# A hybrid decoder layer on one core: the last supertile's gates, keys and mix ahead of the output products, and its output norm by halves

## The chip, the core and the metric

The kernel runs on one core of a Trainium2 chip. The metric is the device time of one launch in microseconds (us). TensorE (PE, with its weight loads as PEld), VectorE (DVE), ScalarE (ACT), GpSimd (POOL) and the DMA queue of SyncE (SP) each work through a list of instructions in a fixed order; semaphores make one engine wait for another. A profiled execution gives start, duration and waits of every instruction.

## The reference

One layer on x of 4096 tokens by 1024 features. From a modulated RMSNorm h, one projection feeds sliding-window attention (window 128), RWKV-7 time mixing and gated linear attention; each is multiplied by its SiLU gate, and the three side by side are the mix.

```python
h = _rmsnorm(x, g_pre) * (1.0 + scale[:, None]) + shift[:, None]
proj = h @ w_in
...
attn = attn * jax.nn.silu(ag)
...
rwkv = rwkv * jax.nn.silu(rg)
gla = _gla_mixer(h, gq, gkk, gv, gk1, gk2, gk_b, gla_norm_w) * jax.nn.silu(gg)
y = jnp.concatenate([attn, rwkv, gla], axis=-1) @ w_out
return x + gate[:, None] * _rmsnorm(y, g_post)
```

## The kernel before

The sequence is cut into NS = 16 supertiles of NT = 256 tokens. A first phase computes h, the RWKV and the linear-attention part and stores them in device memory (hscr, mscr). The second phase, which the change touches, makes attention, gates, mix and output for each supertile i. Products of full precision are split in a high and a low float16 half, and three products of halves stand for one.

The stages of the second phase are Python generators:

- `qkv(i)` projects keys (`kp`), queries (`qp`, two tiles) and values (`vp`) from h (tile `hT`, two buffers).
- `gates(i)` makes four gate tiles (`gp`), 48 matmuls each, and writes tanh and product into the one tile `ag`.
- `stage_s(i)` is the attention in two halves of 128 tokens: scores `sc`, softmax in `pr`, a transpose on DVE, and `ovp`, 40 small matmuls for each group, copied to `mxa`.
- `stage_m(i)` loads the other half of the mix (`mxb` from mscr), multiplies both by the gates, squares them on ACT for a common power-of-two scale (sums by the small matmul `mp`, result `msc`, `oi`), and splits seven combinations of the mix into `block`s. A block is one ACT and one DVE instruction of 512 columns, into one of four slots of `mtp` in turn.
- `outp(i)` runs seven products of 12 matmuls of 512 columns (a seven-product scheme for a two by two block product). Product n reads block n and a weight: four stay in SBUF (`o`), three (n = 0, 3, 6) share `ov`, which is loaded again during the product that reads it, by two DMAs issued after its 6th and 12th matmul. `add` on DVE combines the results from PSUM (tag `pj`, two banks, shared with the projections) into `yv`.
- `norm(i, a, ...)` squares 1024 columns on ACT, takes the inverse root on DVE in small one-column steps, scales, adds x and stores 128 tokens.

`stage_p2(i)` strings them together: outp(i-1), gates(i), load of h, qkv(i+1), and for i = 15 also outp(15). So gates(15) came after outp(14), and outp(15) came when all was done but its own mix. `stage_m(i)` waited until outp(i-1) was emitted as a whole.

The class `Order` notes every instruction with the tiles it reads and writes. Its `pin` then plans the order on each engine by a model of durations: whatever is ready and has the lowest rank (program order, with add and the PSUM read-outs lifted by URGENT = 150) goes next. That order is fixed in the program. The chip follows it, whatever the durations turn out to be.

Where the profile names L334, it is the one line of the class `Lane` through which every operation is issued, so tiles tell operations apart.

Of the kernel before, what the change touches and what calls it, by code (L numbers as in the profile page):

```python
# [21 lines left out]
P = 128  # L22
D = 1024
T = 4096
NT = 256
NS = T // NT
# [9 lines left out]
URGENT = 150  # L36
# [362 lines left out]
def hybrid_kernel(ctx, tc, x, vecs, rows, ada1, adaw, w1, wl, w2, wo, w2aug, a2, gk2, cst, ctr, ctg, abias, out):  # L399
    nc = tc.nc  # L400
    model = Model(tc)
    V = Lane(model, nc.vector, *LANES[0])
    S = Lane(model, nc.scalar, *LANES[1])
    G = Lane(model, nc.gpsimd, *LANES[2])
    PE = Lane(model, nc.tensor, *LANES[3], serial=True)
    SP = Lane(model, nc.sync, *LANES[4])

    def pool_of(at, name, bufs=1, **kw):
        return model.order.pool(at.enter_context(tc.tile_pool(name=name, bufs=bufs, **kw)), bufs)
# [4 lines left out]
    st = pool_of(ctx, "small", 3)  # L414
# [13 lines left out]
    magic = cp.tile([P, 16], I32, name="magic")  # L428
# [60 lines left out]
    def pjt(name):  # L489
        return pst("pj", name, 2)  # L490
# [4 lines left out]
    def mq(name):  # L495
        return pst("mq", name)
# [52 lines left out]
    done = set()  # L549
# [95 lines left out]
    with ExitStack() as p1:  # L645
# [155 lines left out]
        for n in range(2 * KD):  # L801
            k, half = n // 2, n % 2
# [978 lines left out]
    def block(i, n):  # L1781

        f = F[i]
        t = blocks[len(split) % len(blocks)]
        split.append((i, n))
        f["blk"].append(t)
        S.activation(t[:, 0], f["src"][n], AF.Identity, scale=f["msc"])
        V.scalar_tensor_tensor(t[:, 1], f["src"][n], f["msc"], t[:, 0], op0=ALU.mult, op1=ALU.subtract)

    def stage_m(i):  # L1790

        yield [("s", i), ("gates", i), ("o", i - 1)]
        f = F[i]
        ag, half = f["ag"], [f["mx"], wt([P, 4, NT], "mxb", 1)]
        SP.dma_start(half[1].rearrange("p b n -> p (b n)"), mscr[i])
        yield [*half, ag]
        mss = st.tile([P, 2], F32, tag="mss", name="mss")
        f["blk"] = []
        for j in range(2):
            for n in (2 * j, 2 * j + 1):  # L1800
                z = half[j][:, 2 * (n % 2) : 2 * (n % 2) + 2, :].rearrange("p b n -> p (b n)")
                V.scalar_tensor_tensor(z, z, g_h[n], ag[:, 2 * n : 2 * n + 2, :].rearrange("p b n -> p (b n)"),
                                       op0=ALU.mult, op1=ALU.mult)
            S.activation(blocks[(len(split) + j) % len(blocks)].rearrange("p a k n -> p (a k n)"),
                         half[j].rearrange("p k n -> p (k n)"), AF.Square, accum_out=mss[:, j : j + 1])
# [12 lines left out]
        (a11, a21), (a12, a22) = [[h[:, :, t * P : (t + 1) * P] for t in range(2)] for h in half]  # L1818
        s1 = wt([P, 4, P], "sm1", 1)
        f["src"] = [a11, a12, a11, s1, a21, a22, a12]  # L1820
        V.tensor_tensor(s1, a21, a22, op=ALU.add)
        V.tensor_tensor(a21, a11, a21, op=ALU.subtract)
        yield [msc]
        block(i, 0)
        V.tensor_tensor(a11, s1, a11, op=ALU.subtract)
        block(i, 1)
        V.tensor_tensor(a12, a12, a11, op=ALU.subtract)
        yield [a11]
        for n in range(2, len(blocks)):
            block(i, n)  # L1830

    def load_o(t, n):
# [3 lines left out]

    PRODUCTS = ((0, False), (1, True), (6, True), (3, False), (4, True), (5, True), (2, False))

    def outp(i):
# [5 lines left out]
        yv = [wt([P, D], "yv", 2) for _ in range(2)]  # L1845
        c1, c2 = slice(0, 512), slice(512, 1024)

        def product(po, n):
            yield [f["blk"][n]]
            A, (w, stays) = f["blk"][n], PRODUCTS[n]  # L1850
            W = Wr[w] if stays else Wv
            for k in range(KD // 2):
                for a, b in ((0, 0), (0, 1), (1, 0)):
                    PE.matmul(po, A[:, a, k, :], W[:, k, :, b, :], start=k == a == b == 0,
                              stop=k == KD // 2 - 1 and a == 1)
                if k == 1 and not stays:
                    later = [m for m, s in PRODUCTS[n + 1 :] + PRODUCTS[: n + 1] if not s][0]
                    if n < 6 or i < NS - 1:
                        SP.dma_start(Wv[:, 0:2], woscr[later, :, 0:2])
                if k == 3 and not stays and (n < 6 or i < NS - 1):  # L1860
                    SP.dma_start(Wv[:, 2:4], woscr[later, :, 2:4])
                yield
            if n + len(blocks) < 7:
                block(i, n + len(blocks))

        def full(n):
            yield ["pj"]
            po = pjt("op")
            yield from product(po, n)
# [8 lines left out]
        yield from full(0)  # L1878
        model.order.urgent = URGENT
        S.copy(y21, f["po"])  # L1880
        model.order.urgent = 0
        yield from full(1)
        add(y11, y21)
# [5 lines left out]
        add(y22, y12)  # L1889
        add(y21, y21)  # L1890
        yield from full(5)
        add(y21, y21)
        norm(i, 1, yv[1], x2[:, 0:D], f["blk"][5])
        if i < NS - 1:
            SP.dma_start(x2[:, 0:D], x[i * NT : i * NT + P, :])
        else:
            SP.dma_start(x2[:, D : 2 * D], x[i * NT : i * NT + P, :])
        yield from full(6)
        add(y12, y12)
        norm(i, 0, yv[0], x2[:, 0:D] if i < NS - 1 else x2[:, D : 2 * D], f["blk"][6])  # L1900
        done.add(("o", i))

    def norm(i, a, yv, xt, junk):
        oi = F[i]["oi"]
        sy = st.tile([P, 1], F32, tag="sy", name="sy")
        S.activation(junk.rearrange("p a k n -> p (a k n)"), yv, AF.Square, scale=oi, accum_out=sy)
        V.tensor_scalar(sy, sy, 1.0 / D, 1e-6, op0=ALU.mult, op1=ALU.add)
        ry = st.tile([P, 1], F32, tag="ry", name="ry")
        rsqrt(ry, sy, 1)
        V.tensor_mul(ry, ry, oi)  # L1910
        V.scalar_tensor_tensor(yv, yv, ry, gn, op0=ALU.mult, op1=ALU.mult)
        V.tensor_add(yv, yv, xt)
# [197 lines left out]
```

## Time and profile before

| | |
|---|---|
| runs of the kernel | 2110.41, 2110.42, 2101.18 us, median 2110.41 |
| profiled execution | 2094.68 us, of it the span 2092.9 us |
| mean granted clock of PE | 0.98 |
| one supertile in steady state | 62.5 us |
| DVE busy | 1613.3 us, 77% of the span |

The profile's page gives busy times over the span; the stages differ, so the end of the run has to be read in windows of its own. One supertile of the second phase repeats with little change, as the chain of work that ended last shows in order of time (start, duration, engine, tile): two scores, the products, ovp, gates, ovp, gates, keys, queries.

```profile
1949.62 5.61 PE op L334 x26
1955.23 0.87 PE sc L334 x8
1956.10 8.20 PE op L334 x38
1964.30 1.36 PE ovp L334 x78
1967.51 1.29 PE op L334 x6
1968.80 11.90 PE gp L334 x109
1980.70 1.36 PE ovp L334 x78
1982.06 9.17 PE gp L334 x83
1991.23 2.62 PE kp L334 x24
1993.85 5.25 PE qp L334 x48
```

All steps but a few are PE's. The chain follows the wait that ended last, so the engines not in it had finished earlier.

### The profile page before, as it was taken

Reading aid. Unit: us, or ns where it says so; the run is one execution under the profiler, and the core shown is the slowest. Engines: PE = TensorE matmul, PEld = TensorE weight load, DVE = VectorE, ACT = ScalarE, POOL = GpSimd, SP = SyncE. Lnnn points to the kernel's source line nnn. Section 1 sums busy time; section 2 is a strip of 40 time slices with the busy share of each in tenths; the row PEclk is TensorE's granted clock in tenths of the full one; section 3 lists DMA queues with packets and bytes.
Section 4 is the critical chain, followed back from the end, with each engine's and each line's share of the span. In section 5 each row is a group of like instructions: output and inputs, shape, how many; then the busy total and the mean of one; then the engine's idle time right before and its main releaser. Section 6 shows DMA issues by size and latency. Waiting matters only on the chain. (4 is left out here: it accounts for less than half of the span.)

```text
span 2092.9 us, 61576 instructions
## 1 busy us (share of the span) xinstructions
PE 1957.4 (94%) x24931; PEld 1517.7 (73%) x24931; DVE 1613.3 (77%) x5214; ACT 1152.2 (55%) x2758; POOL 214.3 (10%) x403
## 2 busy tenths in 40 slices
PE   5899999999999999999876999999999999999996
PEld 2678777787787778777666677777787777787773
DVE  5777888878877688988736878877778877777876
ACT  4867676576776766765334444443444453444442
POOL 0520111421111112101100000000000000000000
PEclk9999999999999999999988999999999999999998
DMA  8432233323323322445034434333334343334341
GB/s 328 137 94 78 74 105 98 92 91 109 97 81 116 102 66 66 116 152 166 20 90 161 154 122 144 105 129 110 124 112 144 106 135 105 122 112 144 116 133 71
DMA packets 183606, 241.95 MB, mean 116 GB/s; under 512 B 52163, under 2 KB 141716, under 8 KB 179094
## 3 DMA queue, kind: packets, MB, share of 16 engines
q1 hardware_dynamic: 183174, 237.45, 35.2%
q8 instruction: 197, 3.23, 0.7%
q14 instruction: 91, 0.75, 0.1%
q10 hardware_dynamic: 144, 0.52, 0.1%
HBM read 177.08 MB, written 60.82 MB: 114 GB/s over the span
## 5 line engine op out<-in xcount | busy, mean ns | idle before, releaser
L334 PEld LDWEIGHTS <-mtp 128*128 128x128 f16 x1344 | 130.4, 98 | 142.5 <-issue 3.8
L334 PE MATMUL op<-o,mtp 128*128 128x512 f16 x768 | 171.9, 380 | 0.0
L334 ACT ACTIVATE pr<-pr,nm,lsc 128x256 f32<-128x256 f32 (+1 forms) x256 | 149.2, 585 | 36.7 <-DVE nm L334 36.7
L334 PE MATMUL op<-ov,mtp 128*128 128x512 f16 x576 | 144.9, 381 | 2.1 <-ACT mtp L334 2.1
L334 PEld LDWEIGHTS <-hT 128*128 128x128 f16 x1536 | 119.4, 100 | 25.4 <-issue 4.0
L334 DVE TENSOR_TENSOR yv<-op,yv 128x512 f32<-128x512 f32 x112 | 75.1, 681 | 56.6 <-PE op L334 41.3
L334 DVE CUSTOM_DVE_ANT_0 pr<-sc,ab,sinks 128x256 f32<-128x256 f32 (+1 forms) x256 | 107.8, 475 | 8.8 <-PE sc L334 6.0
L334 ACT ACTIVATE mtp<-yv,oi 128x1024 f16<-128x1024 f32 x32 | 36.6, 1144 | 126.7 <-DVE yv L334 125.2
L334 PE MATMUL pv<-gvh,hT 128*128 128x272 f16 x512 | 99.4, 285 | 6.1 <-DVE kg L334 3.0
L334 ACT ACTIVATE ag<-gp,gh 128x512 f32<-128x512 f32 x64 | 43.7, 683 | 106.6 <-PE gp L334 106.6
L334 POOL COPY kT<-kT 128x512 f16<-128x512 f16 x15 | 9.7, 647 | 869.8 <-DVE kT L334 820.4
L334 PE MATMUL lp<-hT,Lh 128*128 128x256 f16 x512 | 92.4, 274 | 0.1
L334 PE MATMUL gp<-hT,q3h 128*128 128x256 f16 x512 | 87.1, 275 | 4.3 <-PEq L1967 3.9
L334 DVE SCALAR_TENSOR_TENSOR ag<-ag,gp 128x512 f32<-128x512 f32 x64 | 43.8, 685 | 61.3 <-ACT ag L334 61.3
L334 PE MATMUL gp<-hT,q5h 128*128 128x256 f16 x512 | 90.1, 277 | 0.1
L334 PE MATMUL zz<-hT,vh 128*128 128x256 f16 x512 | 88.8, 273 | 1.3 <-DVE zb L334 1.3
L334 PE MATMUL zz<-hT,kh 128*128 128x256 f16 x512 | 89.8, 273 | 0.0
L334 PE MATMUL zz<-hT,rh 128*128 128x256 f16 x512 | 89.8, 275 | 0.0
L334 PE MATMUL gqk<-hT,gqkh 128*128 128x256 f16 x512 | 89.6, 276 | 0.0
L334 PE MATMUL qp<-hT,q0h 128*128 128x256 f16 x512 | 85.3, 273 | 2.3 <-DVE yv L334 1.5
L334 PE MATMUL qp<-hT,q1h 128*128 128x256 f16 x512 | 86.2, 273 | 0.0
L334 PE MATMUL gp<-hT,q4h 128*128 128x256 f16 x512 | 85.2, 273 | 0.0
(438 smaller groups left out, 6029.4 us busy)
## 6 DMA issues: line engine op xcount, KB each, us to landing
ov<-woscr SPq DMA_DIRECT2D x96, 512.0 KB, 3.9
xt<-in_x SPq DMA_DIRECT2D x16, 1024.0 KB, 5.0
hscr<-hT SPq DMA_DIRECT2D x16, 1024.0 KB, 5.4
hT<-hscr SPq DMA_DIRECT2D x16, 1024.0 KB, 4.8
out<-yv SPq DMA_DIRECT2D x32, 512.0 KB, 2.9
x<-in_x SPq DMA_DIRECT2D x30, 512.0 KB, 4.3
cs<-in_w SPq DMA_DIRECT2D x112, 128.0 KB, 2.3
v<-vscr SPq DMA_DIRECT2D x128, 64.0 KB, 2.5
```

The lines of the kernel that those rows point to most:

```text
L334: r = f(*args, **kw)
```

## The change

The order of stages is changed for the last supertiles only. stage_p2(14) runs outp(13), qkv(15), gates(14); stage_p2(15) runs gates(15), outp(14), outp(15). stage_m(15) waits for the mix of 14 and not for all products of 14; before its blocks it waits for the products of 14 whose slots it takes. It gets buffers that are free by then: `mxe` in a slot of hT in place of mxb, `pr` tiles for the squares, and `q` tiles in place of yv. outp(15) runs product 1 ahead of product 0 and makes blocks 4 and 5 after product 0.

The last norm is rewritten. `last_square` squares 512 columns as soon as they are complete and multiplies them by gn at once. `last_norm` takes the inverse root with two small instructions for a step in place of three, scales and adds x by halves of 512 columns, and stores four pieces in place of two. For the second 128 tokens (h = 1) the scaling is on ACT and the add of x on POOL.

```diff
-        yield [("s", i), ("gates", i), ("o", i - 1)]
+        yield [("s", i), ("gates", i), ("o" if i < NS - 1 else "m", i - 1)]
         f = F[i]
-        ag, half = f["ag"], [f["mx"], wt([P, 4, NT], "mxb", 1)]
+        ag, half = f["ag"], [f["mx"], wt([P, 4, NT], "mxb", 1) if i < NS - 1 else
+                              t_hT("mxe").rearrange("p a k n -> p (a k n)").bitcast(F32)[:, 0 : 4 * NT].rearrange("p (b n) -> p b n", b=4)]
...
+        def last(n):
+            return [(f"o{n}", i - 1)] if i == NS - 1 else []
...
-        yield [msc]
+        yield [msc, *last(3)]
         block(i, 0)
         V.tensor_tensor(a11, s1, a11, op=ALU.subtract)
+        if i == NS - 1:
+            yield last(4)
         block(i, 1)
...
+            if i == NS - 1:
+                yield last(n + 3)
             block(i, n)
...
+    def last_square(f, h, part, sums):
+
+        z = f["end"][h]
+        cols = slice(part * 512, part * 512 + 512)
+        S.activation(f["junk"][:, 0:512], f["yv"][h][:, cols], AF.Square, scale=f["oi32"], accum_out=sums[:, part : part + 1])
+        V.tensor_tensor(z[:, cols], f["yv"][h][:, cols], gn[:, cols], op=ALU.mult)
+
+    def last_norm(f, h, sums, xt):
+
+        v, y, t = [st.tile([P, 1], F32, tag=f"ln{n}", name=f"ln{n}") for n in range(3)]
+        V.scalar_tensor_tensor(v, sums[:, 0:1], 1e-6, sums[:, 1:2], op0=ALU.add, op1=ALU.add)
+        V.tensor_single_scalar(t.bitcast(I32), v.bitcast(I32), 1, op=ALU.logical_shift_right)
+        V.tensor_tensor(y.bitcast(I32), magic[:, 0:1], t.bitcast(I32), op=ALU.subtract)
+        for c in (3.0, 12.0, 768.0):
+            V.scalar_tensor_tensor(t, y, y, v, op0=ALU.mult, op1=ALU.mult)
+            V.scalar_tensor_tensor(y, t, -c, y, op0=ALU.add, op1=ALU.mult)
+        V.scalar_tensor_tensor(y, y, -1.0 / 8192, f["oi"], op0=ALU.mult, op1=ALU.mult)
+        z, r0 = f["end"][h], (NS - 1) * NT + h * P
+        for cols in (slice(0, 512), slice(512, 1024)):
+            if h:
+                S.activation(z[:, cols], z[:, cols], AF.Identity, scale=y)
+                G.tensor_tensor(z[:, cols], z[:, cols], xt[:, cols], op=ALU.add)
+            else:
+                V.scalar_tensor_tensor(z[:, cols], z[:, cols], y, xt[:, cols], op0=ALU.mult, op1=ALU.add)
+            SP.dma_start(out[r0 : r0 + P, cols], z[:, cols])
...
-            if n + len(blocks) < 7:
-                block(i, n + len(blocks))
+            for m in ((4, 5), ())[n] if i == NS - 1 and n < 2 else (n + len(blocks),) if n + len(blocks) < 7 else ():
+                block(i, m)
+            done.add((f"o{n}", i))
...
+        first = [(y21, 0)] if not end else [(y11, 1), (y21, 0)]
+        for y, n in first:
+            yield from full(n)
+            model.order.urgent = URGENT
+            S.copy(y, f["po"])
+            model.order.urgent = 0
+        if end:
+            add(y11, y11)
+            last_square(f, 0, 0, sums[0])
...
-        if i == 1:
+        if i in (1, NS - 1):
             yield from gates(i)
         if i > 0:
             yield from outp(i - 1)
-        if i > 1:
+        if i == NS - 2:
+            yield from qkv(i + 1)
+        if 1 < i < NS - 1:
             yield from gates(i)
```

Where the order moves, first on PE, before, at the start of the last products (op is a product's PSUM tile, q6l the low half of a gate weight, gp of 15):

```order
L334 MATMUL gp_33795<-hT_32198,q6l_18742 128x256
L334 MATMUL mp_33857<-mss_33850,ones_64 128x2
L334 LDWEIGHTS mtp_21671
L334 MATMUL op_33889<-ov_19576,mtp_21671 128x512
L334 LDWEIGHTS mtp_21671
```

The same place with the change: the end of gates(15), then, where the dots are, the first two products of supertile 14, and the mp of 15.

```order
L334 MATMUL gp_33638<-hT_32198,q6l_18742 128x256
L334 LDWEIGHTS mtp_21671
L334 MATMUL op_33694<-ov_19576,mtp_21671 128x512
...
L334 MATMUL op_33721<-o1_19572,mtp_21671 128x512
L334 MATMUL mp_33728<-mss_33705,ones_64 128x2
L334 LDWEIGHTS mtp_21671
L334 MATMUL op_33757<-o6_19573,mtp_21671 128x512
```

So mp of 15 stood alone between the last gate and the first product; now it stands between products 1 and 2 of supertile 14.

Next DVE after outp(13), at the softmax of 14's second half, as a piece of the difference (pr is the softmax tile, kT and kp the keys of 15, q and qp its queries, sy the norm's sum):

```order
 L334 TENSOR_TENSOR yv<-yv,x_21670 128x1024
+L334 SCALAR_TENSOR_TENSOR kT<-kp,kq_s,kT 64x256 x4
 L334 TENSOR_TENSOR sm<-sm,es 128x8
 L334 RECIPROCAL rd<-sm 128x8
-L334 TENSOR_SCALAR pr<-pr,rd 128x256 x4
-L334 SCALAR_TENSOR_TENSOR ag<-ag,gp 128x512
-L334 TENSOR_SCALAR pr<-pr,rd 128x256 x4
+L334 TENSOR_SCALAR sy<-sy 128x1
+L334 TENSOR_SCALAR pr<-pr,rd 128x256 x8
 L334 STREAM_TRANSPOSE pr<-pr 128x1024 x2
+L334 SCALAR_TENSOR_TENSOR q<-qp,q 64x512
```

The keys moved ahead of the softmax's scaling, and the queries behind its transposes.

Last DVE with the change between the products of 14 and of 15 (yv_33693 and 33692 are the halves of 14 in its norm, q_33889 and q_33890 those of 15, op_33912 is product 0 of 15 and op_33935 its product 2):

```order
L334 SCALAR_TENSOR_TENSOR mtp_21671<-sm1_33745,msc_33732,mtp_21671 128x512
L334 SCALAR_TENSOR_TENSOR yv_33693<-yv_33693,ry_33827,x2_21670 128x1024
L334 SCALAR_TENSOR_TENSOR nwt_33869<-nwt_33869,sy_33864 128x1
L334 SCALAR_TENSOR_TENSOR mtp_21671<-mxe_33690,msc_33732,mtp_21671 128x512
L334 TENSOR_TENSOR yv_33693<-yv_33693,x2_21670 128x1024
L334 SCALAR_TENSOR_TENSOR ry_33867<-nwt_33869,ry_33867 128x1
L334 TENSOR_TENSOR nwt_33869<-ry_33867 128x1
L334 SCALAR_TENSOR_TENSOR nwt_33869<-nwt_33869,sy_33864 128x1
L334 SCALAR_TENSOR_TENSOR mtp_21671<-mxa_33048,msc_33732,mtp_21671 128x512
L334 TENSOR_TENSOR q_33889<-op_33912,q_33889 128x512
```

The blocks and adds of 15 now stand among the norms of 14, which before lay under the gates of 15. Between the seventh add of 14 and the add of op_33912 there are 23 rows; these nine are the last, and the 14 ahead of them are one more block (of mxa) and 13 rows of one column.

On SP the load of `mxe` now waits for gates(14) to have read hT, the two loads of x for the end wait for gates(15), and the loads of ov stand behind them. The store of 14's second half stands ahead of the ov loads of 15's last product.

More of the change, by code (lines that the diff above doesn't have):

```diff
@@ L1803, in stage_m @@
                                        op0=ALU.mult, op1=ALU.mult)
-            S.activation(blocks[(len(split) + j) % len(blocks)].rearrange("p a k n -> p (a k n)"),
-                         half[j].rearrange("p k n -> p (k n)"), AF.Square, accum_out=mss[:, j : j + 1])
+            if i < NS - 1:
+                junk = blocks[(len(split) + j) % len(blocks)].rearrange("p a k n -> p (a k n)")
+            else:
+                junk = wt([P, 4, 256], "pr", 3).rearrange("p j n -> p (j n)").bitcast(F16)[:, 0:D]
+            S.activation(junk, half[j].rearrange("p k n -> p (k n)"), AF.Square, accum_out=mss[:, j : j + 1])
         done.add(("og", i))
@@ L1837, in hybrid_kernel @@
     PRODUCTS = ((0, False), (1, True), (6, True), (3, False), (4, True), (5, True), (2, False))
+    def last_square(f, h, part, sums):
[17 more added lines that the diff above has]
+                G.tensor_tensor(z[:, cols], z[:, cols], xt[:, cols], op=ALU.add)
+            else:
+                V.scalar_tensor_tensor(z[:, cols], z[:, cols], y, xt[:, cols], op0=ALU.mult, op1=ALU.add)
+            SP.dma_start(out[r0 : r0 + P, cols], z[:, cols])
     def outp(i):
@@ L1844, in outp @@
         yield [("m", i)]
-        yv = [wt([P, D], "yv", 2) for _ in range(2)]
+        yv = [wt([P, D], "yv", 2) if i < NS - 1 else
+              wt([P, 2, 4, NT], "q", 2, F16).rearrange("p a b n -> p (a b n)").bitcast(F32) for _ in range(2)]
         c1, c2 = slice(0, 512), slice(512, 1024)
@@ L1877, in outp @@
         (y11, y12), (y21, y22) = [[y[:, c1], y[:, c2]] for y in yv]
[L1878 to L1883, printed above, removed]
+        end = i == NS - 1
+        if end:
+            f["yv"], (f["junk"], *f["end"]) = yv, [wt([P, 4, 256], "pr", 3).rearrange("p j n -> p (j n)") for _ in range(3)]
+            oi32 = f["oi32"] = st.tile([P, 1], F32, tag="oi32", name="oi32")
+            V.tensor_single_scalar(oi32, f["oi"], 1.0 / 32, op=ALU.mult)
+            sums = [st.tile([P, 2], F32, tag="lsum", name="lsum") for _ in range(2)]
+        first = [(y21, 0)] if not end else [(y11, 1), (y21, 0)]
[4 more added lines that the diff above has]
+            model.order.urgent = 0
+        if end:
+            add(y11, y11)
+            last_square(f, 0, 0, sums[0])
+        else:
+            yield from full(1)
+            add(y11, y21)
         yield from full(2)
@@ L1889, in outp @@
         add(y22, y12)
+        if end:
+            last_square(f, 1, 1, sums[1])
         add(y21, y21)
@@ L1892, in outp @@
         add(y21, y21)
-        norm(i, 1, yv[1], x2[:, 0:D], f["blk"][5])
-        if i < NS - 1:
+        if end:
+            last_square(f, 1, 0, sums[1])
+            last_norm(f, 1, sums[1], x2[:, 0:D])
+            SP.dma_start(x2[:, D : 2 * D], x[i * NT : i * NT + P, :])
+        else:
+            norm(i, 1, yv[1], x2[:, 0:D], f["blk"][5])
             SP.dma_start(x2[:, 0:D], x[i * NT : i * NT + P, :])
-        else:
-            SP.dma_start(x2[:, D : 2 * D], x[i * NT : i * NT + P, :])
         yield from full(6)
         add(y12, y12)
-        norm(i, 0, yv[0], x2[:, 0:D] if i < NS - 1 else x2[:, D : 2 * D], f["blk"][6])
+        if end:
+            last_square(f, 0, 1, sums[0])
+            last_norm(f, 0, sums[0], x2[:, D : 2 * D])
+        else:
+            norm(i, 0, yv[0], x2[:, 0:D], f["blk"][6])
         done.add(("o", i))
```

## The prediction

> **What bounds the kernel now.** I read the page first, then the last 125 us as windows, then the waits in them, then single rows. The first two lines are the page's; in the windows the columns are length, then busy time and instructions of each engine, then TensorE's granted clock.
>
> ```profile
> span 2092.9 us, 61576 instructions
> PE 1957.4 (94%) x24931; PEld 1517.7 (73%) x24931; DVE 1613.3 (77%) x5214; ACT 1152.2 (55%) x2758; POOL 214.3 (10%) x403
> ```
> ```profile
> 1968.64:2031.12 62.48, 61.60 (x640) 46.93 (x639) 48.88 (x136) 27.98 (x71) 0.00 (x0) 1.00 0.37 121
> 2031.12:2053.70 22.58, 22.58 (x273) 19.79 (x271) 17.93 (x49) 9.88 (x28) 0.00 (x0) 1.00 0.33 113
> 2053.70:2059.83 6.13, 0.60 (x3) 0.50 (x3) 4.11 (x14) 2.61 (x5) 0.00 (x0) 0.68 0.00 0
> 2059.83:2079.56 19.73, 19.73 (x84) 8.42 (x84) 10.65 (x18) 5.78 (x9) 0.00 (x0) 0.93 0.32 106
> 2079.56:2092.90 13.34, 0.00 (x1) 0.00 (x0) 8.77 (x29) 1.24 (x2) 0.00 (x0) 0.64 0.19 79
> ```
> ```profile
> PE mp L334 <- ACT mtp L334: 3.5, 1, 3.5
> PE op L334 <- ACT mtp L334: 2.1, 1, 2.1
> PE sc L334 <- DVE m L334: 0.9, 1, 0.9
> ```
>
> PE bounds the run: up to 2053.70 it is busy all the time but 0.9 us. Then supertile 15 has nothing to hide behind: PE stands for 6.13 us while the mix is formed, runs the 84 product matmuls, and the last 13.34 us are norm and store with PE empty. The change can gain only in these three stretches; elsewhere PE's work is the same, since both kernels have the same matmuls and the orders agree up to 1968.64, where product 6 of supertile 13 has been issued.
>
> **The change, part by part.**
>
> *1. The gap in front of the products.* Product 0 of 15 now comes after the products of 14, during which stage_m(15) runs. PE keeps only the small product mp, 0.14 us between busy neighbours: 6.13 − 0.14 = **6.0 us** go.
>
> ```profile
> 2059.83 1.03 PE L334 MATMUL op<-ov,mtp 128*128 128x512 f16 x2 [2.07 <-ACT mtp L334]
> 2060.66 1.06 PE L334 MATMUL op<-o,mtp 128*128 128x512 f16 x2
> 2061.51 2.94 PE L334 MATMUL op<-ov,mtp 128*128 128x512 f16 x10
> 2064.29 4.91 PE L334 MATMUL op<-o,mtp 128*128 128x512 f16 x22
> ```
> ```profile
> 2059.83:2063.50 3.67, 3.67 (x11) 0.60 0.00 0
> 2063.50:2070.00 6.50, 6.50 (x32) 1.00 0.48 161
> ```
>
> *2. The slow first matmuls.* After the gap the first two start 0.42 us apart; 14 take 2064.29 − 2059.83 = 4.46 us. The next 22 take 4.75 (to 2069.04, where the next group starts), 0.216 each, so 14 should take 3.02. The granted clock is 0.60 here and 1.00 later. Without the gap this **1.4 us** goes too. The wait of sc for DVE (0.9 us, in supertile 14's scores) goes as well, because these scores now lie among gate matmuls. A PE without new waits would thus end 6.0 + 1.4 + 0.9 = 8.3 us earlier, at 2079.56 − 8.3 = 2071.2.
>
> *3. New waits at the softmax.* From here times are before's scale. (Timeline rows: start, duration, engine, line, operation; group rows: busy us and mean ns behind the bar.) The ovp of 14's second half now stands on PE behind kp and two qp products: 24 + 96 matmuls at 0.109 us from 1968.64, so PE gets there at 1981.7. On DVE the four kT rows now stand ahead of its softmax.
>
> ```profile
> 1972.34 1.23 DVE L334 TENSOR_TENSOR yv<-yv,x 128x1024 f32<-128x1024 f32 x1
> ...
> 1974.19 1.14 DVE L334 TENSOR_SCALAR pr<-pr,rd 128x256 f32<-128x256 f32 x4
> ...
> 1976.90 2.52 DVE L334 STREAM_TRANSPOSE pr<-pr 128x1024 f32<-128x1024 f32 x2
> ```
> ```profile
> L334 DVE SCALAR_TENSOR_TENSOR kT<-kp,kq_s,kT 64x256 f16<-64x256 f32 x64 | 30.9, 482 | 23.9 <-ACT kT L334 23.4
> L334 ACT ACTIVATE kT<-kp,kq_s 64x256 f16<-64x256 f32 x64 | 29.8, 466 | 21.0 <-DVE kT L334 15.2 <-PE kp L334 5.3
> ```
>
> From 1973.5: two kT on DVE (1.0), two on ACT in between (0.9), two on DVE (1.0), three small rows (0.6), eight scalings (2.2), two transposes (2.5): 1981.7. That is a tie; I take 0.3 us of waiting, and 0.2 for qp's bank, which is read out behind the transposes. The two ovp of 15 have about a microsecond to spare by the same rows. Bounds 0 and 1.5 us; behind a waiting ovp all of PE waits.
>
> *4. A new wait at product 3 of 15.* It needs the PSUM bank of product 0, which the DVE frees with an add. Between the last add of 14 and this one DVE now has (the order quoted above): one add, four low halves of blocks, the scaling and the add of 14's norm over 1024 columns, and 17 rows of one column.
>
> ```profile
> L334 DVE TENSOR_TENSOR yv<-op,yv 128x512 f32<-128x512 f32 x112 | 75.1, 681 | 56.6 <-PE op L334 41.3 <-issue 15.1
> L334 DVE SCALAR_TENSOR_TENSOR mtp<-mxa,msc,mtp 128x512 f16<-128x512 f32 x48 | 35.9, 749 | 8.9 <-ACT mtp L334 8.5
> ```
> ```profile
> 2074.42 1.29 DVE L334 TENSOR_TENSOR yv<-op,yv 128x512 f32<-128x512 f32 x2 [1.90 <-PE op L334]
> ...
> 2086.25 0.16 DVE L334 TENSOR_TENSOR ry<-ry,oi 128x1 f32<-128x1 f32 x1
> 2086.45 1.28 DVE L334 SCALAR_TENSOR_TENSOR yv<-yv,ry,x 128x1024 f32<-128x1024 f32 x1
> 2087.76 1.22 DVE L334 TENSOR_TENSOR yv<-yv,xo 128x1024 f32<-128x1024 f32 x1
> ```
>
> Two adds of 0.68 take 1.29 back to back, so a row costs some 0.07 less than it lasts: 0.62 + 4 × 0.68 + 1.2 + 1.15; the 17 small rows are 0.19 apart in one chain (2086.25 to 2086.45) and about half that where two chains alternate, say 0.14, 2.4 us. Sum 8.1, then the add itself 0.65: the bank is free 8.85 us after product 6 of 14 ends. PE has three products before it, 36 × 0.216 = 7.8. Wait **1.1 us**; with small rows at 0.08 or 0.19 it is 0.1 or 1.9. The loads of ov behind it: issued after matmuls 6 and 12 of product 6, landing 3.9 us later, used 3.9 and 4.5 us after issue, so just in time; 0.2 us for these and mp. Sum of new waits 0.3 + 0.2 + 1.1 + 0.2 = 1.8 us: PE ends at 2071.2 + 1.8 = **2073.0**.
>
> *5. The end.* Before, PE's end to the span's end is 13.34 us.
>
> ```profile
> 2077.80 1.15 ACT L334 ACTIVATE mtp<-yv,oi 128x1024 f16<-128x1024 f32 x1 [8.05 <-DVE yv L334]
> ...
> 2079.07 0.15 DVE L334 TENSOR_SCALAR sy<-sy 128x1 f32<-128x1 f32 x1 [1.37 <-ACT mtp L334]
> ...
> 2084.62 4.73 SPq L334 DMA_DIRECT2D out<-yv  x2
> ```
> ```profile
> L334 ACT ACTIVATE osq<-osb 128x512 f32<-128x512 f32 x16 | 10.1, 629 | 0.6
> L334 POOL TENSOR_TENSOR qb<-qg,bdm x32: 1046/1050/1613, 103.6 to 987.4; 128x512 f32<-128x512 f32 x32
> DMA to landing us min/median/max: 2.6/2.9/3.8
> mscr<-osb SPq DMA_DIRECT2D x16, 256.0 KB, 2.6
> ov<-woscr SPq DMA_DIRECT2D x96, 512.0 KB, 3.9
> ```
>
> Now, counted from PE's end: last add to 0.7; square over 512 columns instead of 1024, 0.8 to 1.65 (the 1024 one took 1.27 to its reader; osq shows 0.63 for 512); ten small rows with those of the other half between them to 3.7; two scalings of 512 to 5.05. The other half goes by ACT (from 2.2, twice 0.65) and POOL (twice 1.1) to 5.3. The multiplications by gn (four of 0.62 on DVE) lie under the products and, the last, beside ACT's square; without that cover each costs 0.6. The four stores go out one behind another, the last at 5.4; before, the last was issued at 2089.01 and the span ended 3.9 us later. For 256 KB instead of 512 I take 0.3 less (2.6 against 2.9; bounds 0 and 0.6), and 0.3 more because four overlap (bounds 0 and 0.6). So 5.4 + 3.9 = **9.3** instead of 13.34; bounds 8.8 and, with both POOL adds at 1.61, 10.4.
>
> Sum: 2073.0 + 9.3 = 2082.3, that is 10.6 us less than 2092.9. Bounds: 0.2 us of waits and 8.8 give 12.9 less; 3.7 and 10.4 give 7.6 less. The profiled execution took 2094.68 us (its span and 1.8 around it); the three runs shown took 2101.18 to 2110.42, median 2110.41. I take 10.6 off the median: **2099.8 us**.
>
> **A rule against it.** POOL's adds run beside DVE operations on two SBUF inputs; among such neighbours qb above varies from 1.05 to 1.61 us. The Trainium skill, GPSIMD Engine Reference, section "Key points", says that GpSimd shares its SBUF interfaces with VectorE and contends with DVE instructions that have two SBUF inputs; by it they take 1.61 us here and the sum is 9.5 us instead of 10.6. The third rival below prices this from the row.
>
> **The rivals.**
> - *No new wait bites*: everything in 3 and 4 is covered. 12.7 less, 2097.7 us. For: the ties are within 0.3 us. Against: the DVE has 8.1 us of work in 7.8 of PE's.
> - *DVE becomes the bound of the last 38 us.* It has adds, blocks, both norms of 14 and gn there, some 32 us of rows. If each wait for another engine adds 0.1 us that no product covers, some 3 to 4 us come on top: 7 less, 2103.4 us. For: the wait in 4 is of this kind. Against: in the window 2031.12 to 2053.70 DVE is busy 17.93 of 22.58 and PE never waits.
> - *POOL's adds at 1.61 us*: 2 × 0.5 later, 9.5 less, 2100.9 us.
> - *The mix doesn't get ahead*: m(15) still waits for the blocks of 14, and 1 and 2 come back in part; only the tail's 4 us are won, 2106.4 us. Against: blocks 0 to 3 of 15 take slots that products 3 to 6 of 14 free, and each is read two products later.
> - *Slower*: three times an ovp stands on PE, with everything behind it, for transposes that DVE reaches late behind keys and gates. Each such stop also slows the matmuls after it, 1.4 us as in 2. Above 10.6 us in all, 2.1 us of waiting each, the kernel is slower; with 6 us each it loses 22.2 and gains 10.6, so 2122.0 us. For: the ovp are in PE's order where DVE is just done. Against: by 3 the first is a tie, and the other two have slack.
>
> **How the numbers follow.** About 0.5%, 10.5 us, is what a measurement of this kernel can tell from no change, and the forecast lies on that line. Forecast 0.62, half of it on either side (0.32 and 0.30); no wait 0.13, faster; DVE bound 0.14, POOL 0.06 and mix not ahead 0.03, all within 0.5%; slower 0.02. Faster 0.45, same 0.53, slower 0.02. The range reaches up to DVE as the bound, and 1.6 more for its own unknowns, 2105.0; down it takes in that a run of the same kernel can be 9.2 us under the median (2101.18): 2101.18 − 12.9 = 2088.3, so 2088.0. Left out are the mix rival, slower, and medians near the profiled execution's time.
>
> **What would show it.** Right: PE without a gap over 0.5 us from 1968 to its end but one of about a microsecond before op<-ov of product 3; no 0.42-us matmuls; granted clock 1.00 to the last product; PE's end at 2073, 9.3 us before the span's end. Wrong: ovp rows with idle time ascribed to DVE pr; op rows waiting for DVE q more than once; POOL adds of 1.6 us; a last store later than 5.4 us after the last matmul.

## The result and the profile after

| | before | after |
|---|---|---|
| runs beside each other (19 each), median | 2102.9 us (2098.29 to 2110.42) | 2094.66 us (2088.46 to 2101.07) |
| ratio, 95% interval | | 0.9957, 0.9946 to 0.9968 |
| profiled execution, of it the span | 2094.68 us, 2092.9 us | 2093.64 us, 2091.8 us |
| PE's part: from the place where the orders part to PE's end | 110.92 us | 104.03 us |
| PE's end to the span's end | 13.34 us | 11.05 us |

By the ratio the change gains 0.43%, 9.0 us of 2102.9 (6.7 to 11.4 by the interval); the two medians differ by 8.2. The two profiled spans differ by 1.1 us only, for a reason outside the change: in the execution of after, the second phase began 8.0 us later. The tile `fi` shows it, the one value that every engine loads between the phases (columns: duration, then start).

```profile
L2013 PEldq TENSOR_LOAD <-fi x1: 487/487/487, 1129.1 to 1129.1; - x1
```

Before, that load stood at 1121.1. In the traces of the experiments, whose first phase is the same, it stood anywhere from 1124.3 to 1135.0 (leaving out the one execution of 6807 us told below). From there to PE's end it is 958.46 us before and 951.65 after. So everything below is measured from places in the program, not from the span's start: PE's part from the place where the orders part (1968.64 before; after, the first keys matmul of supertile 15, 1976.72) to the end of its last matmul, called E (2079.56 and 2080.75), and the tail from E to the span's end.

First PE's part of after, as windows (length, busy time and instructions of PE, PEld, DVE, ACT, POOL; granted clock; DMA), then from the waits the first of its two, and the row that shows the second:

```profile
1976.72:2043.30 66.58, 66.07 (x828) 58.44 (x827) 51.35 (x144) 32.37 (x90) 0.00 (x0) 1.00 0.20 65
2043.30:2080.75 37.45, 36.87 (x172) 16.54 (x169) 30.68 (x77) 16.08 (x28) 0.00 (x0) 1.00 0.60 211
```
```profile
PE gp L334 <- DVE q L334: 0.5, 1, 0.5
```
```profile
2070.24 1.46 PE L334 MATMUL op<-ov,mtp 128*128 128x512 f16 x6 [0.46 <-DVE q L334]
```

PE is busy for 102.94 of 104.03 us (66.07 + 36.87 of 66.58 + 37.45) at clock 1.00. The gap of 6.13 us, the 0.42-us matmuls and the wait of `sc` are not there. What is left are half a microsecond behind the bank of `qp` at the first gates, and 0.46 us in front of product 3 of 15.

Then the tail of after, as a timeline (the bracket holds the idle time ahead, and what ended it):

```profile
2083.03 3.23 DVE L334 SCALAR_TENSOR_TENSOR ln<-ln,ln 128x1 f32<-128x1 f32 x6
2086.29 0.16 DVE L334 SCALAR_TENSOR_TENSOR ln<-ln,oi 128x1 f32<-128x1 f32 x1
2086.49 1.42 DVE L334 SCALAR_TENSOR_TENSOR pr<-pr,ln,xo 128x512 f32<-128x512 f32 x2
2088.36 0.40 SPq L334 DMA_DIRECT2D out<-pr  x1
```

Six one-column rows on DVE take 3.23 us, where 0.2 us each were expected. The single rows behind that group:

```profile
2083.73 0.16 DVE L334 SCALAR_TENSOR_TENSOR ln<-ln,ln 128x1 f32<-128x1 f32 x1
2083.93 1.11 DVE L334 SCALAR_TENSOR_TENSOR ln<-ln,ln 128x1 f32<-128x1 f32 x1
2085.07 1.18 DVE L334 SCALAR_TENSOR_TENSOR ln<-ln,ln 128x1 f32<-128x1 f32 x1
```
```profile
2083.76 1.26 POOL L334 TENSOR_TENSOR pr<-pr,xo 128x512 f32<-128x512 f32 x1 [138.83 <-ACT pr L334]
2084.99 1.25 POOL L334 TENSOR_TENSOR pr<-pr,xo 128x512 f32<-128x512 f32 x1
```

The DVE rows are quick until POOL starts. The next one ends at 2085.04, where POOL's first add ends (2085.02), and the one after it at 2086.25, where the second ends (2086.24). Both read two tensors in SBUF. That suggested the theory which the first runs test: a DVE row with two SBUF inputs is held while POOL adds. The trace of before already held such rows, in its first phase:

```profile
L334 DVE SCALAR_TENSOR_TENSOR ch<-cs,wsc,ch x56: 443/479/1266, 127.2 to 650.4; 128x256 f16<-128x256 f32 x56
```

Of these rows, with two inputs in SBUF and a median of 479 ns, the one that starts at 395.25 takes 1.26 us; POOL's qb, the row that the prediction took its price from, runs beside it from 395.00 to 396.23.

The tail has a second, smaller loss, in SP's order. SP waits once for POOL and twice for DVE in it, and for the fourth store not at all:

```profile
SPq L334 <- POOL pr L334: 8.5, 1, 8.5
SPq L334 <- DVE pr L334: 2.2, 2, 1.9
```

So the last store, issued at 2088.36, must be that of POOL's second half, ready since 2086.24; it stands behind both stores of the other half, the last of which left at 2087.93.

### The profile page after: what moved, and what is told of

Read it like the earlier page. It is cut to its first block, busy times and chain, and to the rows that moved or that the text cites. A ratio compares the mean times of both kernels' runs of the same rounds, so it can differ in the third digit from the quotient of the medians.

```text
span 2091.8 us, 61571 instructions
## 1 busy us (share of the span) xinstructions
PE 1961.3 (94%) x24931; PEld 1521.0 (73%) x24931; DVE 1612.5 (77%) x5211; ACT 1154.3 (55%) x2765; POOL 216.3 (10%) x405
## 3 DMA queue, kind: packets, MB, share of 16 engines
q8 instruction: 197, 3.23, 0.6%
## 5 line engine op out<-in xcount | busy, mean ns | idle before, releaser
L334 DVE TENSOR_TENSOR yv<-op,yv 128x512 f32<-128x512 f32 x105 | 70.4, 681 | 48.6 <-PE op L334 34.3
L334 PE MATMUL gp<-hT,q6h 128*128 128x256 f16 x512 | 85.3, 273 | 0.0
```

Of the source, the lines that this page charges most:

```text
L334: r = f(*args, **kw)
```

## The experiments

E is the end of PE's last matmul. All kernels are made from the changed one, except where that is said.

**Without POOL's adds.**

```diff
                 S.activation(z[:, cols], z[:, cols], AF.Identity, scale=y)
-                G.tensor_tensor(z[:, cols], z[:, cols], xt[:, cols], op=ALU.add)
```

> From the changed kernel; left out: the add of x for the last 128 tokens (the two POOL rows pr<-pr,xo of 128x512), so their output lacks x; ACT's scalings stay. Theory A, in the changed kernel's tail the one-column DVE rows with two SBUF inputs are held until the end of a POOL add (two rows of about 1.15 us, 2.0 us in all): without the adds the six rows ln<-ln,ln that took 3.23 us take 1.1 to 1.2 us, and from PE's end to the span's end it is 9.0 us (8.7 to 9.3) instead of 11.05. Rival B, the rows are held by something else at that time (ACT's two scalings, the stores, or waits among the rows): the six rows stay at 3.2 us and the tail at 11.0.

The same DVE rows in its timeline:

```profile
2082.14 1.31 DVE L334 SCALAR_TENSOR_TENSOR ln<-ln,ln 128x1 f32<-128x1 f32 x6
2083.48 0.16 DVE L334 SCALAR_TENSOR_TENSOR ln<-ln,oi 128x1 f32<-128x1 f32 x1
2083.68 1.41 DVE L334 SCALAR_TENSOR_TENSOR pr<-pr,ln,xo 128x512 f32<-128x512 f32 x2
```

The six rows take 1.31 us instead of 3.23, with ACT's scalings still beside them. E is 2079.86; the wide rows end at E + 5.23 (after: E + 7.16), the tail is 8.44 us, 2.6 less. That is more than the hold of 1.93 us (7.16 less 5.23). The store that stood last is now out early, so the last one is issued at 2085.12, E + 5.26, as soon as its data are there; that is 0.43 us more. From there to the end it takes 3.2 us instead of 3.4. POOL's adds are what held the rows; the rival falls.

**Rows with one tensor input.**

```diff
-            V.scalar_tensor_tensor(t, y, y, v, op0=ALU.mult, op1=ALU.mult)
-            V.scalar_tensor_tensor(y, t, -c, y, op0=ALU.add, op1=ALU.mult)
-        V.scalar_tensor_tensor(y, y, -1.0 / 8192, f["oi"], op0=ALU.mult, op1=ALU.mult)
+            V.tensor_scalar(t, y, y, v, op0=ALU.mult, op1=ALU.mult)
+            V.tensor_scalar(y, t, -c, y, op0=ALU.add, op1=ALU.mult)
+        V.tensor_scalar(y, y, -1.0 / 8192, f["oi"], op0=ALU.mult, op1=ALU.mult)
```

> From the changed kernel, everything computed; the one-column steps of the inverse root are tensor_scalar with v, y and oi as scalar operands (one tensor input each) instead of scalar_tensor_tensor with two. Theory A (a DVE row with two SBUF tensor inputs is held while POOL adds, one with a single tensor input is not): the seven rows take 1.3 to 1.5 us in all with none over 0.3, although POOL's adds lie beside them; the first 512-column row (two SBUF inputs) is held instead, to the end of a POOL add; tail 10.2 to 10.8 us. Variant A2 (any DVE row is held while POOL adds): two rows of about 1.15 us as before, tail 11.0.

The first execution took 6807.21 us: PE ran at about a third of its speed from the first matmul on (741 ns instead of 273 for one of the gates). What slowed it is open. The kernel was therefore run again.

> The kernel of one_input_rows again, since in its execution PE ran at about a third of its speed from the first matmul on (741 ns for a gates matmul instead of 273), which no row of the edit explains. Theory A: span about 2091 us; the seven one-column rows 1.9 us in all with none over 0.3, the first 512-column row held to the end of the second POOL add (1.8 us instead of 0.7), tail 10.4 to 10.8 us. Rival: the slow PE comes from the edit: span near 6800 us again.

The second took 2096.11 us, so the slow PE doesn't come with the edit. Its tail:

```profile
2085.99 1.64 DVE L334 TENSOR_SCALAR ln<-ln,ln 128x1 f32<-128x1 f32 x6
2086.73 2.48 POOL L334 TENSOR_TENSOR pr<-pr,xo 128x512 f32<-128x512 f32 x2 [139.34 <-ACT pr L334]
...
2087.92 2.50 DVE L334 SCALAR_TENSOR_TENSOR pr<-pr,ln,xo 128x512 f32<-128x512 f32 x2
```
```profile
L334 DVE SCALAR_TENSOR_TENSOR pr<-pr,ln,xo x2: 739/1288/1837, 2087.9 to 2089.7; 128x512 f32<-128x512 f32 x2
```

No one-column row is over 0.28 us, though POOL adds from 2086.73 on. The first row with two SBUF inputs behind them takes 1.84 us instead of 0.75: it starts at 2087.92 and ends at 2089.76, half a microsecond after POOL's second add (2089.21). So it is the two inputs that are held. The first execution shows the same rows: 1.64 us for the six, beside 2.48 of POOL, and 2.50 for the two wide ones. Little is won: the tail is 10.9 us, just above what was expected, since six of these rows take 1.64 us instead of 1.31 and the hold is only passed on to the next row.

**POOL's adds in quarters.**

```diff
-                G.tensor_tensor(z[:, cols], z[:, cols], xt[:, cols], op=ALU.add)
+                for q in (slice(cols.start, cols.start + 256), slice(cols.start + 256, cols.stop)):
+                    G.tensor_tensor(z[:, q], z[:, q], xt[:, q], op=ALU.add)
```

> From the changed kernel, everything computed; each of the two POOL adds of 512 columns is made as two of 256. Theory A1 (a DVE row waits for the end of the POOL row that runs, and gets through between two of them): four rows are held about 0.5 to 0.6 us each instead of two of 1.15, together 2.0 to 2.4 us over the normal 0.19, tail 10.9 to 11.4. Theory A3 (a held row costs about 1 us whatever the size of the POOL row): four rows of about 1.1 us, tail about 13. Rival B (not POOL): two rows of 1.15 us as in the changed kernel.

Single rows of DVE, then POOL's:

```profile
2089.79 0.57 DVE L334 SCALAR_TENSOR_TENSOR ln<-ln,ln 128x1 f32<-128x1 f32 x1
2090.39 0.65 DVE L334 SCALAR_TENSOR_TENSOR ln<-ln,ln 128x1 f32<-128x1 f32 x1
2091.07 0.65 DVE L334 SCALAR_TENSOR_TENSOR ln<-ln,oi 128x1 f32<-128x1 f32 x1
```
```profile
2089.62 0.73 POOL L334 TENSOR_TENSOR pr<-pr,xo 128x256 f32<-128x256 f32 x1 [138.84 <-ACT pr L334]
2090.30 0.72 POOL L334 TENSOR_TENSOR pr<-pr,xo 128x256 f32<-128x256 f32 x1
2090.99 0.72 POOL L334 TENSOR_TENSOR pr<-pr,xo 128x256 f32<-128x256 f32 x1
```

Four rows are held, these three and the first wide one, and each of the three ends within 0.03 us of a POOL row's end (2090.35, 2091.02, 2091.71): one DVE row gets through for each POOL row. A held row costs what is left of the POOL row, no fixed price. DVE's last row ends at E + 6.99, 0.2 us earlier than in the changed kernel. Yet the tail, 11.59 us, is a little above the 10.9 to 11.4 expected, for a reason in the stores: the first one in SP's order waits here for DVE, so none leaves before 2092.96, the last is issued at 2094.38, E + 7.77, and from there to the end it takes 3.8 us instead of 3.4.

**No POOL at all: both halves on DVE.**

```diff
-            if h:
-                S.activation(z[:, cols], z[:, cols], AF.Identity, scale=y)
-                G.tensor_tensor(z[:, cols], z[:, cols], xt[:, cols], op=ALU.add)
-            else:
-                V.scalar_tensor_tensor(z[:, cols], z[:, cols], y, xt[:, cols], op0=ALU.mult, op1=ALU.add)
+            V.scalar_tensor_tensor(z[:, cols], z[:, cols], y, xt[:, cols], op0=ALU.mult, op1=ALU.add)
```

> From the changed kernel, everything computed; the second 128 tokens get scale and x in two DVE rows of 512 columns like the first, so neither ACT's two scalings nor POOL's two adds are there. The two rows stand in front of six small rows of the other half on DVE. Theory A: DVE gets 1.35 us of work and loses 2.05 us of holding; 512-column rows of the first half end 6.2 to 6.4 us behind PE's end instead of 7.16, last store issued at 6.8, tail 10.1 to 10.3 us instead of 11.05. Rival B (POOL is not the cause): the 1.35 us come on top, tail 12.4.

```profile
2079.55 1.30 DVE L334 SCALAR_TENSOR_TENSOR ln<-ln,ln 128x1 f32<-128x1 f32 x6
...
2081.08 1.41 DVE L334 SCALAR_TENSOR_TENSOR pr<-pr,ln,xo 128x512 f32<-128x512 f32 x2
```

E is 2076.01: the last rows end at E + 6.48, the tail is 9.69 us. That is below the 10.1 to 10.3 expected: the last store is issued at 2082.52, E + 6.51, where 6.8 was expected, and the end follows 3.2 us later (3.4 in the changed kernel). DVE does more work and is done 0.7 us earlier. To see whether the runs tell it from the changed kernel, it was timed twice, the second time beside the changed kernel on one chip.

> The kernel of dve_adds again, timed in rounds: the second 128 tokens get scale and x in two DVE rows, no POOL adds; everything computed. By the traces it ends 1.35 us ahead of the changed kernel (tail 9.7 instead of 11.05) and 10.5 us ahead of before: ratio 0.9950 (0.994 to 0.996). Rival: the gain in the tail is an accident of one execution, ratio 0.9957 like the changed kernel.

> The kernel of dve_adds (no POOL adds; everything computed) timed beside the changed kernel on the same chip. By the traces 1.35 us less than the changed kernel: ratio to before 0.9950 against 0.9957. Rival: no difference that the runs can tell.

> The changed kernel as it is, timed beside dve_adds_more on the same chip. Ratio to before 0.9957 (0.9946 to 0.9968); in its trace two one-column DVE rows of 1.1 to 1.2 us beside POOL's adds, tail 11.05 us, kp to PE's end 104.0 to 104.2 us.

| | ratio to before | tail in its trace |
|---|---|---|
| dve_adds_timed | 0.9947 (0.9928 to 0.9967) | 9.72 us |
| dve_adds_more | 0.9941 (0.9925 to 0.9957) | 9.75 us |
| changed_again | 0.9947 (0.9931 to 0.9963) | 11.22 us |

Three traces agree on a tail 1.3 to 1.5 us shorter. The runs point the same way (0.0006 on one chip, 1.3 us), but their intervals overlap, so they don't show it. By its traces it is the shortest version that computes everything.

**The parts apart.** First the new order with the old norm (where the dots stand, the early squares of the new norm and their buffers go too):

```diff
...
         if end:
-            last_square(f, 1, 0, sums[1])
-            last_norm(f, 1, sums[1], x2[:, 0:D])
+            norm(i, 1, yv[1], x2[:, 0:D], f["blk"][5])
...
-            last_square(f, 0, 1, sums[0])
-            last_norm(f, 0, sums[0], x2[:, D : 2 * D])
+            norm(i, 0, yv[0], x2[:, D : 2 * D], f["blk"][6])
```

> The new order of stages and the new buffers with the norm of before for supertile 15 (squares over 1024 columns, its steps of the inverse root, two stores of 512 KB); everything computed. Theory: the two parts of the change add up. From the first keys matmul (kp) of 15 to PE's end 104.0 us as in the changed kernel (103.8 to 104.4; 110.92 from the same place in the program before), granted clock 1.00 to the end, tail 13.3 us (13.0 to 13.6) as before. So 6.9 us less than before, ratio 0.9967. Rival: the early squares and multiplications of the new norm were what loaded DVE at product 3, and without them its wait goes: 103.5 us; or the old norm's tail grows behind the new order, above 13.6.

```profile
1971.79:2075.84 104.05, 103.16 (x997) 74.81 (x995) 79.86 (x215) 47.37 (x113) 0.00 (x0) 1.00 0.35 118
```

In this one window of PE's part the clock is 1.00 and PE is idle for 0.89 us in all, without the gap of 6.13: ratio 0.9964 (0.9948 to 0.998), PE's part 104.05 us, tail 13.36. Then the kernel before with the new norm at its end (its functions and buffers, as in the change, stand where the dots are):

```diff
...
-        norm(i, 1, yv[1], x2[:, 0:D], f["blk"][5])
+        if end:
+            last_square(f, 1, 0, sums[1])
+            last_norm(f, 1, sums[1], x2[:, 0:D])
+        else:
+            norm(i, 1, yv[1], x2[:, 0:D], f["blk"][5])
...
-        norm(i, 0, yv[0], x2[:, 0:D] if i < NS - 1 else x2[:, D : 2 * D], f["blk"][6])
+        if end:
+            last_square(f, 0, 1, sums[0])
+            last_norm(f, 0, sums[0], x2[:, D : 2 * D])
+        else:
+            norm(i, 0, yv[0], x2[:, 0:D], f["blk"][6])
```

> The order of stages of before with the new norm for supertile 15; everything computed. Theory: the tail is that of the changed kernel, 11.05 us (10.8 to 11.4), with two one-column rows held by POOL's adds; PE's gap of 6.13 us in front of the products and its slow first matmuls are there as before, 110.9 us from the same place in the program. So 2.3 us less than before, ratio 0.9989. Rival: the hold comes from the new order (something else that runs late beside the tail): then no row is held here, tail 9.0 to 9.3 us, ratio 0.998.

```profile
2085.11 3.23 DVE L334 SCALAR_TENSOR_TENSOR ln<-ln,ln 128x1 f32<-128x1 f32 x6
```

The hold is the same 3.23 us: ratio 0.9989 (0.9973 to 1.0004), tail 11.26 us; the two waits of the gap are there (3.5 and 2.1 us). In the traces the order is worth 6.9 us and the norm 2.1 to 2.3, and they add up. The runs agree (7.6 and 2.3 us of 2102), though norm_only alone isn't told from no change.

One number differs from before: the 84 products behind the gap take 20.81 us here, and took 19.73 there.

```profile
2061.84:2066.90 5.06, 5.05 (x12) 1.75 (x13) 4.11 (x6) 1.90 (x3) 0.00 (x0) 0.50 0.09 19
```

The clock is at 0.50 for the first 5.06 us of them. Before, it was back at 1.00 from 2062.76 on, 2.93 us after the first product. So what the slow matmuls cost depends on the execution.

**The wait of product 3.** The first attempt left out the wide rows of 14's norm:

```diff
-        V.scalar_tensor_tensor(yv, yv, ry, gn, op0=ALU.mult, op1=ALU.mult)
-        V.tensor_add(yv, yv, xt)
+        if i != NS - 2:
+            V.scalar_tensor_tensor(yv, yv, ry, gn, op0=ALU.mult, op1=ALU.mult)
+            V.tensor_add(yv, yv, xt)
```

> From the changed kernel; left out: the two wide DVE rows of supertile 14's norm (scaling by the inverse root and gn, and the add of x, over 1024 columns, for both halves), so the output of its 256 tokens is wrong. Theory: product 3 of 15 waits 0.46 us since DVE is behind with 14's work: without 2.35 us of wide rows ahead of the add, the wait is gone (0 us), and kp to PE's end is 103.5 us instead of 104.03. Rival: PE waits there for the load of ov, or for another row: the wait stays at 0.2 us or more. The wait at the gates (0.5 us behind qp's bank, 50 us earlier) stays in both.

The wait for DVE is gone, but PE's part is 107.40 us, 3.4 longer, and the experiment says nothing on product 3. SP's rows, from the DMA issues those of `ov` from 2058 to 2063 (number, KB each, us to landing), and the windows around PE's stop tell what came in:

```profile
2057.82 0.34 SPq L334 DMA_DIRECT2D out<-yv  x1
2058.39 1.61 SPq L334 DMA_DIRECT2D ov<-woscr  x2
2060.52 0.34 SPq L334 DMA_DIRECT2D out<-yv  x1
```
```profile
ov<-woscr SPq DMA_DIRECT2D x2, 512.0 KB, 6.0
```
```profile
2062.24:2064.44 2.20, 0.00 (x1) 0.00 (x0) 2.13 (x11) 1.37 (x3) 0.00 (x0) 1.00 0.92 307
2064.44:2065.52 1.08, 1.08 (x5) 0.50 (x6) 0.86 (x6) 0.00 (x0) 0.00 (x0) 1.00 0.94 383
2065.52:2068.93 3.41, 3.41 (x9) 1.18 (x8) 0.00 (x0) 0.00 (x0) 0.00 (x0) 0.50 0.49 190
2068.93:2070.00 1.07, 1.07 (x6) 0.49 (x5) 0.00 (x0) 0.64 (x2) 0.00 (x0) 1.00 0.00 0
```

With the rows gone, 14's two stores come earlier in SP's order (in the changed kernel they leave at 2068.47 and 2076.22); they now go out on either side of the two loads of `ov` for product 0 of 15. The first of these, issued at 2058.39, lands 6.0 us later instead of some 4, and PE starts again then. That the stores are what delays it is read from this, not tested apart. PE stands for 2.20 us, and then the clock falls. So the second attempt kept every engine's order and shortened one row alone:

```diff
...
-        V.scalar_tensor_tensor(yv, yv, ry, gn, op0=ALU.mult, op1=ALU.mult)
+        w = slice(0, P) if i == NS - 2 and a == 1 else slice(0, D)
+        V.scalar_tensor_tensor(yv[:, w], yv[:, w], ry, gn[:, w], op0=ALU.mult, op1=ALU.mult, full=[yv, yv, ry, gn])
```

(`full` gives the planner the old sizes; the dots stand for the place where it takes them.)

> The changed kernel with every engine's order kept; one DVE row is shorter: the scaling in supertile 14's norm (yv<-yv,ry,x of the second 128 tokens) takes 128 of its 1024 columns, so these tokens' output is wrong. It stands ahead of the add q<-op,q that frees the bank for product 3 of 15, and gives DVE 1.0 us. Theory: DVE is behind there, so the wait of product 3 for DVE (0.46 us) goes to 0; what is late next is the block mtp<-mxa that waits for ACT, or the load of ov, both within 0.5 us, so kp to PE's end falls from 104.03 to 103.6 to 104.0 us. Rival: PE waits there for the load of ov (or the add waits for product 0 itself): the wait stays at 0.4 to 0.5 us and 104.0.

```profile
2064.37 0.75 DVE L334 SCALAR_TENSOR_TENSOR mtp<-mxa,msc,mtp 128x512 f16<-128x512 f32 x1 [0.72 <-ACT mtp L334]
2065.78 1.46 PE L334 MATMUL op<-ov,mtp 128*128 128x512 f16 x6
```
```profile
PEld L334 <- DMA ov<-woscr: 0.5, 1, 0.5
```

Product 3 no longer waits for DVE, which now itself waits 0.72 us for ACT. Yet PE's part is 103.90 us, only 0.13 less than 104.03: PEld's wait for a load of `ov` ahead of it is 0.5 us where it was 0.3, and PE lost some 0.3 us there. The wait itself also comes and goes without the edit. In changed_again PE waited 0.24 us for a load of `ov` ahead of product 3, product 3 itself did not wait, and PE's part was 104.18. So these runs don't single out one cause of the 0.46 us. They show that several things are due there within half a microsecond.

## Why the prediction was right, and where it was not

The forecast was 10.6 us less, with faster and no change nearly even; measured were 9.0 (6.7 to 11.4), and 9.2 in the trace (6.9 in PE's part, 2.3 in the tail). The median of 2094.66 us lies in the range; that it is 5 us below the forecast of 2099.8 comes from the base, since the three runs shown had a median of 2110.41 and 19 runs have 2102.9. The runs tell this 0.43% from no change, where the prediction put the limit at 0.5%. That the gain is so near the forecast is in part luck: the tail gained 1.7 us less than was put, PE's part 0.3 more.

- **Gap and slow matmuls (6.0 and 1.4 us): right.** order_only, without the new norm, has PE's part at 104.05 us and clock 1.00. But 1.4 us is the price of one execution: behind the same gap the products of norm_only took 1.1 us longer.
- **New waits (1.8 us): too high, by 0.7.** PE's idle time in its part is 1.1 us. PE's part was put at 104.36 us and took 104.03; it is so near because PE's work took 102.94 where the prediction's terms leave 102.6 (110.92 less 8.3), and where these 0.3 us lie isn't known. No `ovp` waited (0.3 predicted), the bank of `qp` cost 0.5 (0.2 predicted). Product 3 waited for DVE as described, but 0.46 us instead of 1.1. The loads of `ov` set the price of the place too: in short_row14 DVE is early and they are due, and in changed_again they take the place of DVE without any edit.
- **DVE as the bound and the stop at ovp: did not come.** Each would have shown as several DVE waits on PE; there are two, of half a microsecond. Nor did the mix stay behind, which would have left a part of the gap.
- **The tail (9.3 us): mis-sized, it took 11.05, beyond its bound of 10.4.** One of the signs of being wrong came, a last store later than 5.4 us. The step that failed is "ten small rows with those of the other half between them to 3.7". Without POOL's adds that step is right (the factor is ready at E + 3.78), and so is the next one (5.05 predicted, 5.23 measured). With them the factor is ready at E + 5.70. The prediction had seen that POOL and DVE share something, but put the price on POOL, as adds of 1.61 us. POOL's adds took 1.26 and 1.25 us; DVE paid, with two rows of 1.11 and 1.18 us on the very chain that ends the run. The last store left at E + 7.61 instead of 5.4; in no_pool_add it left at E + 5.26, and of the 2.35 us between, 1.93 are the hold (7.16 against 5.23) and 0.43 the store's place in SP's order (2088.36 against 2087.93). On the other side, from that issue to the end it took 3.44 us instead of 3.9. So the tail gained 2.3 us where 4.0 were forecast. The rival with POOL's adds at 1.61 us named 9.5 us, near the 9.0 measured, but for a reason that did not occur: the adds were quick.
- **Sums.** 8.1 and 0.65 in part 4 make 8.75 and not 8.85, so that wait should be 1.0. Without any new wait the gain is 10.6 + 1.8 = 12.4 us, not 12.7, and with the low bounds 12.7, not 12.9. None of these moves the account.

The Trainium skill, SBUF — State Buffer, sections "SBUF: two separate sides" and "Who interferes with whom", says this more sharply than its GPSIMD Engine Reference, quoted in the prediction: VectorE and GpSimd share one pair of ports as an exclusive lock, held for a whole instruction by the one that starts first, the other blocks fully, and a VectorE instruction with one SBUF input, outside the modes that use both ports, stays out of it. The runs agree where GpSimd comes first: the ends at 2085.04 and 2086.25 beside POOL's, the four holds in quarters, and the one-input rows that pass. That GpSimd is held in its turn no run here tests. POOL's one row of 1.61 us, which the prediction read as the price, may be such a case: in the trace of before it starts at 217.69, and the DVE row `hT<-hf,hT` beside it, with two inputs, takes 0.67 us where the median of these is 0.68.

## What to carry to other kernels

Giving half of a short final step to GpSimd did not pay here: a chain of one-column VectorE rows with two tensor inputs in SBUF stands still for as long as GpSimd adds, rows with one input pass but hand the hold to the next row with two, and doing all of it on VectorE was some 1.4 us shorter in the traces. When the dependent chain is bounded, cost each row of it against what runs at that moment on the other engines, and look at which finished store stands last in the queue. Where several things are due at the same place within half a microsecond, taking one away gains almost nothing (0.13 us here), and moving stores ahead can cost more than the wait did (3.4 us here).

## What was not expected of the hardware

PE's clock fell to half after stops shorter than 3.4 us, but not after each of them. In no_wide_norm14 the granted clock was still 1.00 during PE's stop of 2.20 us and for about a microsecond after it, fell to 0.50 at 2065.52 and was back at 1.00 from 2068.93 on; the matmuls lost about 1.7 us beside the 2.2 of the stop. The Trainium skill, TensorE: Matmul & The Clock Gate, section "What's actually happening", states an idle window of about 3.4 us for the fall; here shorter stops did it.

The length of a stop does not decide alone, as the first phase shows. A stop of 1.90 us in after, from 634.36 on, was followed by the first of these rows; next come one of 2.34 us and what followed it.

```profile
637.59:644.42 6.83, 5.77 (x100) 3.96 (x99) 1.54 (x4) 1.52 (x4) 1.98 (x4) 0.50 0.22 63
902.22:904.56 2.34, 0.00 (x1) 0.00 (x1) 0.68 (x3) 0.60 (x2) 0.00 (x0) 1.00 1.08 417
904.56:910.00 5.44, 5.44 (x101) 4.11 (x101) 5.37 (x21) 4.81 (x13) 0.30 (x1) 1.00 0.51 172
```

Before, PE stopped for 1.90 us too at that first place of the program, from 631.75 on, and this followed:

```profile
633.65:640.00 6.35, 4.71 (x173) 3.83 (x175) 1.97 (x5) 1.55 (x4) 1.57 (x3) 1.00 0.26 74
```

A stop of 1.90 us was followed by the fall in after and not before, and one of 2.34 us was not. The times of the falls tell more. In each trace they lie whole multiples of 3.413 us apart, to 0.01 us; before, the falls at 393.64, 1008.04 and 2055.93 are 180 and 307 such steps apart. Counted back from the falls of its trace, the 1.90 us of after lie within one step (634.18 to 637.59), and so do the 2.20 of no_wide_norm14 (2062.11 to 2065.52); the clock falls at the end of it. The 2.34 us are cut by a border at 903.82 into 1.60 and 0.74, and the 1.90 of before by one at 632.58 into 0.83 and 1.07. In all these traces, from 100 us on and without that of 6807 us, every step at clock 1.00 with 2.0 us or more of idle PE was followed by the fall, and none with less than 1.1. What decides between these is open. So the same stop can cost PE its clock in one execution and not in the next, which fits the 1.1 us by which the products of norm_only differ from those of before. This is read from the traces; no run was made to test it.
